# Attention's output projection: upper token tiles finished first, with five weight blocks multiplied ahead

## The chip, the cores and the metric

The kernel runs on one core of one Trainium2 chip. The metric is device time in microseconds (us) for one execution of the whole kernel. Three runs of the kernel before gave 1104.22, 1106.31 and 1106.82 us; their median, 1106.31 us, is the time before.

## What is computed

A trunk of two layers over 512 tokens of width 1024. Each layer is a token mixer and then a SwiGLU feed-forward network (FFN), each between two RMS norms, with a shift, scale and gate that come from a conditioning vector. Layer 0 mixes with a stick-breaking attention, whose output projection `w_o` is the stage of this change:

```python
    for i in range(DEPTH):
        shift, scale, gate = ada_modulation(c, mix_ada_w[i], mix_ada_b[i])
        h = rms_norm(x, mix_pre_g[i]) * (1.0 + scale) + shift
        j = i // N_MIXERS
        if i % N_MIXERS == 0:
            y = stick_breaking_mixer(h, sb_w_qkv[j], sb_w_o[j])
        else:
            y = token_mixing_mixer(h, tm_w_in[j], tm_ln_g[j], tm_w_s[j], tm_b_s[j], tm_w_out[j])
        x = x + gate * rms_norm(y, mix_post_g[i])
        shift, scale, gate = ada_modulation(c, ffn_ada_w[i], ffn_ada_b[i])
        h = rms_norm(x, ffn_pre_g[i]) * (1.0 + scale) + shift
        y = swiglu(h, ffn_w_gate[i], ffn_w_up[i], ffn_w_down[i])
        x = x + gate * rms_norm(y, ffn_post_g[i])
```

## The kernel before

**Numbers.** All is float32. Each operand of a matmul is split into a high part, rounded to the matmul's reduced format, and a low part, the rest. `split` (L128) does this with a copy on ACT (ScalarE) for the high part and a subtraction on DVE (VectorE) for the low one. `mm3` (L120, its matmuls recorded at L109) is the product: high by high, high by low, low by high, three matmuls on PE (TensorE) into one PSUM bank. Weights come by DMA into one of two raw buffers (tile `raw`), and `wemit` splits them into the tiles `wh` and `wl`. A raw buffer is free for the next load once its `wl` is made.

**The ring of weights.** `wget` takes the weights in the fixed order of `stream` and also asks for a few of those behind (its `look`, 3 if nothing else is said). `wtile` gives each a slot in turn: one of five in `wpool`, and, once the attention is over, a sixth in `wpool2`, which is opened only then. Which of the five a tile gets, and when, is for the tile framework's scheduler, which also orders the instructions of each engine where the code doesn't chain them. A slot is written again when the last matmul that reads it is done.

**The projection** (`out_proj`, s=0). The 512 tokens are four tiles of 128, here tile 0 to tile 3; "lower" are tiles 0 and 1, "upper" are 2 and 3. The 1024 rows of `w_o` are eight blocks, here block 0 to block 7. A tile's result needs all eight blocks and lies in two PSUM banks, one for each half of the width (tile `y`). One step is one block, one tile, one half: three matmuls of 512 columns. All eight banks of PSUM hold `y` by the end. As the attention ends with the last of eight head pairs, its generator `filler` puts steps of the projection between its matmuls: `NEARLY` = 4 blocks (0 to 3) for tiles 3 and 2, which are 16 steps, spread by the tables `FILLS` and `LAST`. Then `out_proj` does blocks 0 to 3 for tiles 0 and 1, and then, tile by tile in the order 0, 1, 2, 3, the last four blocks (4 to 7, `J` = 4), and after each tile its boundary.

**The boundary** (`boundary`) of a tile is a chain over three engines: squares of `y` on ACT (`junk`) with their sum, `y` times the gate on DVE (`t<-y,G`), a square root on ACT (`sd`), a reciprocal on DVE, the new `x` on DVE (`x<-t,r,x`), its squares on ACT (`junk<-x`), `x` times the scale on DVE (`t<-x,A`), a second root and reciprocal, the normed row on DVE (`t<-t,r,B`), eight transposes on PE into two banks (`tp`), and for each bank a copy on ACT (`hTh`) and a subtraction on DVE (`hTl`). These two are the FFN's input. For the first two tiles ACT also keeps a plain copy (`c`).

**What follows.** The FFN's first three units (`unit`, f = 0 to 2) are computed for half of the tokens at a time, gate and up, 48 matmuls of 256 columns (tile `gu`). `f0.first()` does the lower half (columns 0 to 255) as soon as tiles 0 and 1 are through; the transposes of the other two tiles stand between these three units. Then come the same three units for the upper half, and then the units f = 3 to 21 as seven products of half size (`seven`; tiles `r1` to `r3`), which read four sums of the input, S1 to S4. `sums` makes all four behind the second pair of tiles, from `c` and from the transposes' banks (`fs` on DVE, `Sh` on ACT, `Sl` on DVE). S1 is the difference of the two halves of the upper tokens' channels; the other three need both halves of the tokens.

Of the kernel before, what the change touches and what calls it, by code (L numbers as in the profile page):

```python
# [13 lines left out]
P = 128  # L14
# [19 lines left out]
def trunk(ctx: ExitStack, tc: tile.TileContext, A: dict, out: bass.AP):  # L34
# [458 lines left out]
    def boundary(s, tt, y, xin, hT, S, tag, mid=None):  # L493
# [26 lines left out]
        for q in range(2):  # L520
# [12 lines left out]
            if S is not None and tt < 2:  # L533
                if tt == 0:
                    S["c", q] = slot(F32, "c", 4, 256)
                act.activation(S["c", q][:, :, tt * P : (tt + 1) * P], a, AF.Copy)
            late.append(a)
        return lambda: sums(S, tt, late)
# [33 lines left out]
    def out_proj(s, nk, get_act, wkey, J, bg, hT, nxt=(), pre=None, S=None, steps=0, bg2=None):  # L572
# [10 lines left out]
        def step(k, tt, a, w, halves=(0, 1)):  # L583
            for hf in halves:
                if k == 0 or k == mid and tt == last:
                    y[tt][hf] = bank("y", "p" if tt == last else "b")
                mm3(
                    y[tt][hf][:],
                    a[0][:, tt * P : (tt + 1) * P], a[1][:, tt * P : (tt + 1) * P],
                    w[0][:, 0, hf * 512 : (hf + 1) * 512],  # L590
                    w[1][:, 0, hf * 512 : (hf + 1) * 512],
                    k == 0 or k == mid and tt == last, k == nk - 1 or k + 1 == mid and tt == last,
                )
# [6 lines left out]
        for k in range(nk - J):  # L600
# [17 lines left out]
        ]  # L618
        sqrt_table()
        xs = {tt: x_load(tt) for tt in range(2)}  # L620
        xin = xs.get
        for tt in range(NT):
            for hf in range(2):
                for k, a, w in tail:
# [5 lines left out]
            if tt < 2:  # L630
                boundary(s, tt, y[tt], xin, hT, S, "p" if last == 0 else "b")
                xs[tt + 2] = x_load(tt + 2)
        evacs, late = [], []
        for n, tt in enumerate((2, 3)):
# [5 lines left out]
            if nxt and tt == 2:  # L640
# [4 lines left out]
                    mid if nxt and tt == 3 else None,  # L645
# [211 lines left out]
    with tc.tile_pool(name="att", bufs=1) as att, tc.tile_pool(name="att2", bufs=2) as att2:  # L857
# [284 lines left out]
    class Ffn:  # L1142
        def __init__(self, s, li, hT, S):
            self.s, self.li, self.hT, self.S = s, li, hT, S
# [29 lines left out]
        def first(self):  # L1174
            return [lambda f=f: self.unit(f, 0, 256, 2) for f in range(NH)]
# [58 lines left out]
        def units(self, bg0):  # L1234
            for f in range(NH):
                self.unit(f, 256, 256)()
# [220 lines left out]
    def gmlp(bg, hT, nhT, nS, nxt):  # L1457
# [219 lines left out]
```

## Time and profile before

| | us |
|---|---|
| runs (median of 3) | 1106.31 (1104.22 to 1106.82) |
| span of the profiled execution, which is its own time here: the profile shows nothing around it | 1104.6 |
| PE busy with matmuls | 1085.9 |
| DVE busy | 945.9 |
| ACT busy | 594.2 |

The last product of the attention ends near 243 us of that span, the projection and its boundaries reach to about 290 us, and the units of seven products begin at 312.4 us. In the lists of instructions the columns are start, duration, engine, line, operation, output and inputs by the program's names, shape, count, and in brackets the idle time just before with what ended it. A duration is longer than the distance to the next instruction of the same engine, since these overlap; where a chain of several is added up, the distance counts.

### The profile page before, as it was taken

To read this page: it belongs to the slowest core of one execution; us is meant where nothing else is said; L and a number is where in the kernel's file an instruction comes from. 1 tells how busy PE (TensorE), PEld (TensorE's weight loads), DVE (VectorE), ACT (ScalarE), POOL (GpSimd) and SP (SyncE) were. 2 spreads that over 40 slices of the span, in tenths; PEclk is the share of its full clock that TensorE was granted. 3 is DMA by queue.
4 is the path that set the end of the run, shared out by engine and by line. 5 is a ranking of instruction groups with operands and counts; after the bars stand their busy time and mean duration, and the time that the engine had idled before them with its cause. 6 is when DMAs were issued, how large, how long until landed. Compare 5 with 4: busy or idle time off the path is not lost.

```text
span 1104.6 us, 18512 instructions
## 1 busy us (share of the span) xinstructions
PE 1085.9 (98%) x7404; PEld 979.0 (89%) x7404; DVE 945.9 (86%) x1248; ACT 594.2 (54%) x982; POOL 29.5 (3%) x53
## 2 busy tenths in 40 slices
PE   6999999999999999999999999999999999999997
PEld 4787788788999999998888889988999999989996
DVE  4988999966989999989866967668979999899997
ACT  6554665665655555554243626426555555565662
POOL 0020100000000000000000000001000000000000
PEclk9999999999999999999999999999999999999999
DMA  8976434304433434359757465334334343333252
GB/s 302 370 226 217 142 116 133 125 11 152 157 112 131 162 119 146 132 197 351 272 191 256 144 205 196 96 116 155 128 117 155 128 159 102 110 115 96 77 187 81
DMA packets 51355, 176.38 MB, mean 160 GB/s; under 512 B 6074, under 2 KB 9146, under 8 KB 51268
## 3 DMA queue, kind: packets, MB, share of 16 engines
q1 hardware_dynamic: 48708, 166.81, 44.6%
q0 software_dynamic: 2560, 8.39, 2.1%
q8 instruction: 58, 0.95, 0.3%
q14 instruction: 29, 0.24, 0.1%
HBM read 164.69 MB, written 8.39 MB: 157 GB/s over the span
## 4 chain that ended last, share of the span: by engine, by line
PE 90%; DVE 4%; DMA 2%; ACT 2%; issue 1%; SPq 0%; DVEq 0%; ACTq 0%
PE r L109 32%; PE y L109 18%; PE pqk L109 7%; PE gu L109 6%; PE v L109 5%; PE X L109 4%; PE u L109 4%; PE Y L109 3%; PE av L109 2%; PE z L109 2%; PE tw L117 1%; PE tp L117 1%; PE Z L109 1%; PE W L109 1%; PE ab L109 1%
## 5 line engine op out<-in xcount | busy, mean ns | idle before, releaser
L87 ACT ACTIVATE wh<-raw 128x1024 fp32r<-128x1024 f32 (+1 forms) x112 | 115.7, 1038 | 130.5 <-PE y L109 39.4
L109 PE MATMUL r<-Sh,wh 128*128 128x256 f32 x608 | 168.1, 276 | 0.5 <-ACT e L87 0.5
L109 PE MATMUL r<-Sh,wl 128*128 128x256 f32 x608 | 167.9, 276 | 0.0
L109 PE MATMUL r<-Sl,wh 128*128 128x256 f32 x608 | 167.9, 276 | 0.0
L109 PE MATMUL y<-wh,as 128*128 128x512 f32 x480 | 149.9, 390 | 0.0
L178 DVE TENSOR_TENSOR wl<-raw,wh 128x1024 fp32r<-128x1024 f32 x87 | 105.8, 1222 | 48.2 <-ACT wh L87 47.6
L109 PEld LDWEIGHTS r<-Sh,wh 128*128 128x128 f32 x608 | 114.1, 188 | 1.0 <-ACT e L87 0.9
L109 PEld LDWEIGHTS r<-Sl,wh 128*128 128x128 f32 x608 | 114.1, 188 | 0.1
L109 PEld LDWEIGHTS r<-Sh,wl 128*128 128x128 f32 x608 | 114.1, 188 | 0.0
L109 PEld LDWEIGHTS y<-wh,as 128*128 128x128 f32 x480 | 90.0, 188 | 18.6
L71 DVE TENSOR_TENSOR wl<-f,wh 128x1024 fp32r<-128x1024 f32 x87 | 103.2, 1220 | 0.0
L87 ACT ACTIVATE wh<-f 128x1024 fp32r<-128x1024 f32 x87 | 91.8, 1055 | 15.3 <-DVE f L71 11.6
L87 ACT ACTIVATE e<-r 128x256 f32<-128x256 f32 x114 | 43.7, 385 | 101.8 <-PE r L109 100.8
L109 PE MATMUL y<-wl,as 128*128 128x512 f32 x240 | 93.7, 391 | 0.0
L109 PE MATMUL r<-hTh,wh 128*128 128x256 f32 x304 | 84.2, 277 | 0.2 <-DVE gu L71 0.2
L109 PE MATMUL r<-hTl,wh 128*128 128x256 f32 x304 | 84.0, 276 | 0.0
L109 PE MATMUL r<-hTh,wl 128*128 128x256 f32 x304 | 84.0, 276 | 0.0
L109 PE MATMUL r<-hTh,b 128*128 128x256 f32 x304 | 57.9, 276 | 0.0
L109 PEld LDWEIGHTS r<-hTh,wh 128*128 128x128 f32 x304 | 57.1, 188 | 0.9 <-DVE gu L71 0.9
L109 PEld LDWEIGHTS r<-hTh,wl 128*128 128x128 f32 x304 | 57.1, 188 | 0.0
L109 PEld LDWEIGHTS r<-hTl,wh 128*128 128x128 f32 x304 | 57.1, 188 | 0.0
L87 ACT ACTIVATE wh<-rawx 128x1024 fp32r<-128x1024 f32 x38 | 40.4, 1063 | 29.8 <-PE r L109 29.0
(262 smaller groups left out, 2937.1 us busy)
## 6 DMA issues: line engine op xcount, KB each, us to landing
rawada<-in_ada SPq DMA_DIRECT2D x80, 512.0 KB, 5.7
rawy<-in_wy SPq DMA_DIRECT2D x38, 512.0 KB, 4.6
rawx<-in_wx SPq DMA_DIRECT2D x38, 512.0 KB, 3.7
raw<-in_wdown SPq DMA_DIRECT2D x22, 512.0 KB, 5.4
raw<-in_wdn SPq DMA_DIRECT2D x22, 512.0 KB, 3.6
raw<-in_wqk SPq DMA_DIRECT2D x16, 512.0 KB, 3.9
ada<-in_ada0p SPq DMA_DIRECT2D x12, 512.0 KB, 6.3
raw<-in_wgu SPq DMA_DIRECT2D x12, 512.0 KB, 3.5
```

What stands on the lines that cost most here:

```text
L71: b = getattr(nc.vector, op)(*args, **kw)
L87: b = nc.scalar.activation(*args, **kw)
L109: b = nc.tensor.matmul(o, l, r, start=start, stop=stop, skip_group_check=True)
L117: last_tp[0] = nc.tensor.transpose(o, i, ident)
L178: last_low[0] = nc.vector.tensor_tensor(l[:], raw[:], h[:].bitcast(F32), ALU.subtract)
```

## The change

The projection of the attention gets a mode `up`.

- `NEARLY` is 5: the attention's last pairs also do block 4 for tiles 3 and 2. That is 20 steps ahead in place of 16, and `LAST` gets four more places.
- `J` is 2, and the order of the tiles is 2, 3, 0, 1. Blocks 4 and 5 are done first (block 4 for tiles 0 and 1 only, where it opens their sums; block 5 for all), then blocks 6 and 7 for tile 2 and for tile 3, and then, for each of tiles 0 and 1, blocks 6 and 7 and behind them blocks 0 to 3 (`early`).
- The FFN's first three units take the upper half of the tokens first (`lo` = 256), the lower half later. The second FFN's stay as they were.
- The plain copies `c` are of the upper tiles. A new `sums_up` makes S1 of a tile right at its upper boundary (one `fs`, one `Sh`, one `Sl`), and S2 to S4 at the lower ones (three of each).

The diff, without its smaller lines:

```diff
+        if lead == (0, 1):
+            return lambda: sums(S, tt, late)
+        return lambda: sums_up(S, tt, late)
+
+    def sums_up(S, tt, a):
+        c = slice(tt % 2 * P, (tt % 2 + 1) * P)
...
+        c0, c1 = [S["c", q][:, :, c] for q in range(2)]
...
+        if tt > 1:
+            dve.tensor_tensor(f[:, 0], c0, c1, ALU.subtract)
+            part("1", f[:, 0])
+            return
...
+        dve.tensor_tensor(f[:, 0], a[0], c0, ALU.subtract)
+        dve.scalar_tensor_tensor(f[:, 1], f[:, 0], -1.0, c1, ALU.mult, ALU.subtract)
+        part("2", f[:, 1])
+        dve.tensor_tensor(g[:, 1], f[:, 1], a[1], ALU.add)
+        part("4", g[:, 1])
+        part("3", f[:, 0])
...
-        for k in range(nk - J):
+        for k in range(npre - 1 if up else 0, nk - J):
...
+        early = [(k, get_act(k), pre["w"][k]) for k in range(npre - 1)] if up else []
         sqrt_table()
-        xs = {tt: x_load(tt) for tt in range(2)}
+        seq = (2, 3, 0, 1) if up else (0, 1, 2, 3)
+        xs = {tt: x_load(tt) for tt in seq[:2]}
         xin = xs.get
-        for tt in range(NT):
+        for n, tt in enumerate(seq):
             for hf in range(2):
-                for k, a, w in tail:
+                for k, a, w in tail + (early if n > 1 else []):
                     step(k, tt, a, w, (hf,))
...
+                if up:
+                    f()
...
-        NEARLY = 4
+        NEARLY = 5
...
-        LAST = (2, 2, 2, 2, 2, 2, 1), (1, 1, 1, 1, 1, 1, 1), (2, 0, 2, 0, 2, 2, 0)
+        LAST = (2, 2, 2, 2, 2, 2, 1), (2, 1, 1, 1, 1, 1, 1), (3, 1, 2, 1, 2, 2, 0)
...
-    f0, f1 = Ffn(1, 0, hT1, S1), Ffn(3, 1, hT3, S3)
+    f0, f1 = Ffn(1, 0, hT1, S1, 256), Ffn(3, 1, hT3, S3, 0)
...
-        4, bg, hT1, f0.first(), early, S1,
+        2, bg, hT1, f0.first(), early, S1, up=True,
```

How this moves instructions is shown at three places. Names carry a number for each tile. Block 4 is `wh_2057` and `wl_2058`, block 5 `wh_2063` and `wl_2064`, block 6 `wh_2069` and `wl_2070` in both kernels; block 7 is `wh_2393` before and `wh_2075` now. The banks of tile 0 are `y_2339` and `y_2343` before, `y_2357` and `y_2361` now; those of tile 1 now `y_2365` and `y_2369`, of tile 2 `y_2255` and `y_2259`, of tile 3 `y_2079` and `y_2111`. `o` is the attention's output, and a bracket names whose counters an instruction waits for.

First place: PE where it goes from block 4 to block 5 behind the attention. Before, block 4 of tile 0 stands behind the 16 steps of blocks 0 to 3 (48 matmuls):

```order
L109 MATMUL y_2339<-wl_2058,o_1905 128x512
L109 MATMUL y_2339<-wh_2057,o_1905 128x512
L109 MATMUL y_2339<-wh_2063,o_2102 128x512 [waits Activation_49]
L109 MATMUL y_2339<-wl_2064,o_2102 128x512 [waits DVE_49]
L109 MATMUL y_2339<-wh_2063,o_2102 128x512
L109 MATMUL y_2339<-wh_2069,o_2240 128x512 [waits Activation_49]
L109 MATMUL y_2339<-wl_2070,o_2240 128x512 [waits DVE_49]
L109 MATMUL y_2339<-wh_2069,o_2240 128x512
L109 MATMUL y_2339<-wh_2393,o_2324 128x512 [waits Activation_49]
L109 MATMUL y_2339<-wl_2394,o_2324 128x512 [waits DVE_49]
```

Now the four steps of block 4 (12 matmuls) stand alone between the attention and block 5; this is their end and the start of block 5:

```order
L109 MATMUL y_2369<-wl_2058,o_1905 128x512
L109 MATMUL y_2369<-wh_2057,o_1905 128x512
L109 MATMUL y_2357<-wh_2063,o_2108 128x512 [waits Activation_49]
L109 MATMUL y_2361<-wh_2063,o_2108 128x512
L109 MATMUL y_2365<-wh_2063,o_2108 128x512
L109 MATMUL y_2369<-wh_2063,o_2108 128x512
L109 MATMUL y_2255<-wh_2063,o_2108 128x512
L109 MATMUL y_2259<-wh_2063,o_2108 128x512
L109 MATMUL y_2357<-wl_2064,o_2108 128x512 [waits DVE_49]
```

Blocks 5, 6 and 7 are now each done for all four tiles one after the other (24 matmuls of block 5, 24 of block 6), with six matmuls by `wh` ahead of the first one by `wl`, where before one tile went through blocks 4 to 7 at a time; blocks 0 to 3 of tiles 0 and 1 come last.

Second place: ACT, which makes these blocks' `wh`, behind the attention's last output `o`. Before (`wh_2399` is the FFN's first weight):

```order
L87 ACTIVATE o_2324<-of_2319 128x512 [waits DVE_49]
L87 ACTIVATE wh_2063<-raw_2061 128x1024 [waits DMAHW2_49,PE_49]
L87 ACTIVATE wh_2069<-raw_2067 128x1024 [waits DMAHW3_49,PE_49]
L87 ACTIVATE wh_2393<-raw_2391 128x1024 [waits DMAHW6_49,PE_49]
L87 ACTIVATE wh_2399<-raw_2397 128x1024 [waits DMAHW7_49,PE_49]
L87 ACTIVATE junk,sq_2438<-y_2339 128x512 [waits PE_49]
```

Now:

```order
L87 ACTIVATE o_2342<-of_2337 128x512 [waits DVE_49]
L87 ACTIVATE wh_2063<-raw_2061 128x1024 [waits DMAHW2_49,PE_49]
L87 ACTIVATE wh_2069<-raw_2067 128x1024 [waits DMAHW3_49,DVE_49,PE_49]
L87 ACTIVATE wh_2075<-raw_2073 128x1024 [waits DMAHW6_49,DVE_49,PE_49]
L87 ACTIVATE junk,sq_2426<-y_2255 128x512 [waits PE_49]
```

The counter of PE that the copy of block 5 waits for stood for the last matmul of block 0 before and stands for the last matmul of block 4 now. The copy of block 6 waited for block 1's last and waits for block 5's last; that of block 7 waited for block 2's and waits for block 6's.

Third place: DVE between the normed row of the first finished tile and that of the second. Before (tile 0, then tile 1):

```order
L71 SCALAR_TENSOR_TENSOR t_2440<-t_2440,r_2458,B_1198 128x1024 [waits DVE_49]
L71 TENSOR_TENSOR t_2512<-y_2347,G_458 128x512 [waits Activation_49]
L71 TENSOR_SCALAR ss_2516<-sq_2510 128x1
L71 TENSOR_TENSOR t_2512<-y_2351,G_458 128x512 [waits Activation_49]
L71 TENSOR_TENSOR hTl_2468<-tp_2462,hTh_2467 128x4x128 [waits Activation_49]
L71 RECIPROCAL r_2520<-sd_2518 128x1 [waits Activation_49]
L71 SCALAR_TENSOR_TENSOR x_2412<-t_2512,r_2520,x_2412 128x1024 [waits DMAHW5_49,DVE_49]
L71 TENSOR_TENSOR hTl_2479<-tp_2473,hTh_2478 128x4x128 [waits Activation_49]
L71 TENSOR_TENSOR t_2512<-x_2412,A_676 128x1024 [waits DVE_49]
L71 RECIPROCAL r_2530<-sd_2528 128x1 [waits Activation_49]
L71 SCALAR_TENSOR_TENSOR t_2512<-t_2512,r_2530,B_1198 128x1024 [waits DVE_49]
```

Now (tile 2, then tile 3; the rows from the second `hTl` of tile 2 on; `wl_2376` and `wl_2406` are the FFN's first two weights):

```order
L71 TENSOR_TENSOR hTl_2467<-tp_2461,hTh_2466 128x4x128 [waits Activation_49]
L71 TENSOR_TENSOR fs_2476<-c_2459,c_2470 128x512 [waits Activation_49]
L71 TENSOR_TENSOR t_2494<-y_2079,G_458 128x512 [waits DVE_49]
L71 TENSOR_TENSOR t_2494<-y_2111,G_458 128x512
L71 TENSOR_TENSOR Sl_2475<-fs_2476,Sh_2474 128x4x128 [waits Activation_49]
L71 SCALAR_TENSOR_TENSOR x_2412<-t_2494,r_2502,x_2412 128x1024 [waits DMAHW5_49,DVE_49]
L178 TENSOR_TENSOR wl_2376<-raw_2373,wh_2375 128x1024 [waits DMAHW7_49,Activation_49]
L178 TENSOR_TENSOR wl_2406<-raw_2403,wh_2405 128x1024 [waits DMAHW0_49,Activation_49]
L71 TENSOR_TENSOR t_2494<-x_2412,A_676 128x1024 [waits DVE_49]
L71 RECIPROCAL r_2512<-sd_2510 128x1 [waits Activation_49]
L71 TENSOR_SCALAR ss_2677<-sq_2671 128x1 [waits Activation_49]
L71 SCALAR_TENSOR_TENSOR t_2494<-t_2494,r_2512,B_1198 128x1024 [waits DVE_49]
```

The second tile's `t<-y,G` stood ahead of the first tile's `hTl` and stands behind both of them and behind the new `fs` of S1; `Sl` of S1 and two weights' `wl` have come between. On PE, the transposes of the second tile had 17 matmuls of `y` between them and the first of the FFN, and now have none; 35 matmuls of `y` stand between the first tile's transposes and the second's, where 25 stood.

More of the change, by code (lines that the diff above doesn't have):

```diff
@@ L584, in step @@
             for hf in halves:
-                if k == 0 or k == mid and tt == last:
+                if k == (npre - 1 if up else 0) or k == mid and tt == last:
                     y[tt][hf] = bank("y", "p" if tt == last else "b")
@@ L591, in step @@
                     w[1][:, 0, hf * 512 : (hf + 1) * 512],
-                    k == 0 or k == mid and tt == last, k == nk - 1 or k + 1 == mid and tt == last,
+                    k == (npre - 1 if up and tt < 2 else 0) or k == mid and tt == last,
+                    k == (npre - 2 if up and tt < 2 else nk - 1) or k + 1 == mid and tt == last,
                 )
@@ L1174, in first @@
         def first(self):
-            return [lambda f=f: self.unit(f, 0, 256, 2) for f in range(NH)]
+            return [lambda f=f: self.unit(f, self.lo, 256, 2) for f in range(NH)]
         def seven(self, f, pending, bg0):
```

39 lines of the change are left out of this document (24 added, 15 removed).

## The prediction

> **What bounds the kernel now.** I read the page's busy shares first, then what PE waited for over the whole span, then two stretches by engine, then the chain of work that ended last around the projection.
>
> ```profile
> PE 1085.9 (98%) x7404; PEld 979.0 (89%) x7404; DVE 945.9 (86%) x1248; ACT 594.2 (54%) x982; POOL 29.5 (3%) x53
> ```
>
> ```profile
> PE tp L117 <- DVE x L71: 8.7, 2, 7.8
> ...
> PE av L109 <- DVE ar L71: 0.8, 1, 0.8
> PE r L109 <- ACT e L87: 0.5, 1, 0.5
> PE av L109 <- ACT ar L87: 0.4, 1, 0.4
> ```
>
> PE is busy for 98% of the span, and the list of its waits (us in total, times, longest) says that the rest is its start (8.7) and little else. Three waits lie near this change: 0.8 and 0.4 in the attention's last pairs, 0.5 in the first unit of seven products. They are all that a better order can win here. Everything else that moves time must be a new wait.
>
> The stretches show who is close behind (us, then busy us of PE, its loads, DVE, ACT):
>
> ```profile
> 257.00:290.00 33.00, 32.95 (x205) 28.90 (x204) 29.25 (x44) 23.21 (x49) 3.12 (x5) 1.00 0.48 165
> ...
> 312.40:500.00 187.60, 187.11 (x1621) 185.68 (x1621) 169.65 (x224) 105.32 (x178) 1.92 (x2) 1.00 0.42 147
> ```
>
> In the boundaries DVE is busy 29.25 of 33 us: PE's matmuls cover its chains, with little to spare. In the units PE idles 0.49 us in 187.6, so time that PE loses earlier isn't given back there.
>
> ```profile
> 243.42 22.23 PE y L109 x98
> 265.68 1.09 PE tp L117 x8
> ...
> 277.46 5.71 PE gu L109 x48
> 283.18 0.87 PE tp L117 x8
> ...
> 290.63 21.88 PE gu L109 x192
> ```
>
> The chain through the projection is PE alone. It gives PE's rates: 22.23/98 = 0.227 us for a matmul of y, 0.87 for the eight transposes of a tile, 5.71 for one of the FFN's first units.
>
> **The change: matmuls ahead.** No matmul is added. Four steps (12 matmuls) go into the attention's last pairs. The step behind the wait of 0.8 gets 0.68 us of new cover (3 x 0.227), that behind the wait of 0.4 gets two steps: of 1.2 us 1.1 are gone. **-1.1.**
>
> **The change: four blocks in one slot.** Blocks 0 to 3 are kept to the end, so four of the five slots are taken while the attention lasts, and blocks 4 to 7, all asked for by then (the last look is 3 beyond block 4), follow one another in the fifth. The order says so too: each copy waits for the last matmul of the block before it, and behind that matmul PE has nothing but this block. Before, the slots came from blocks 0 to 3, with other steps to do. Rows of PE, ACT and DVE of before for one such turn:
>
> ```profile
> 233.73 0.33 PE L109 MATMUL av<-ar,U 128*128 128x128 f32 x1 [0.42 <-ACT ar L87]
> ...
> 245.76 0.62 PE L109 MATMUL y<-wh,o 128*128 128x512 f32 x2
> ```
>
> ```profile
> 233.09 1.05 ACT L87 ACTIVATE ar<-tw,oneb 128x384 fp32r<-128x384 f32 x2
> ...
> 246.19 1.07 ACT L87 ACTIVATE wh<-raw 128x1024 fp32r<-128x1024 f32 x1 [0.28 <-PE y L109]
> ...
> 254.77 1.06 ACT L87 ACTIVATE wh<-raw 128x1024 fp32r<-128x1024 f32 x1 [1.44 <-DMA raw<-in_wgu]
> ```
>
> ```profile
> 247.29 1.23 DVE L178 TENSOR_TENSOR wl<-raw,wh 128x1024 fp32r<-128x1024 f32 x1 [0.33 <-ACT wh L87]
> 250.00 1.23 DVE L178 TENSOR_TENSOR wl<-raw,wh 128x1024 fp32r<-128x1024 f32 x1 [1.49 <-ACT wh L87]
> ```
>
> Block 0's last matmul started at 245.76 and the copy into its slot at 246.19, 0.43 later. PE could start another matmul 0.23 after it, so 0.2 is lost before the copy. The copy takes 1.07. PE follows about 0.1 behind (the first of two `ar`, half of 1.05, ends near 233.63; `av` starts at 233.73). That is 1.37 us for each of blocks 5, 6, 7. The `wl` (ready 0.03 + 1.23 + 0.1 after the copy) is covered by six matmuls by `wh` (1.36). Raw data are no limit: block 7's load starts when block 5's `wl` is made, and one load takes 3.5 us (250.00 + 1.23 to 254.77), against two blocks' 10.9 us of matmuls. **3 x 1.37 = +4.1.**
>
> **The change: boundaries with less cover.** DVE and ACT are idle through those waits, and the first boundary starts late. I follow the chain with time 0 at block 7's first matmul, by distances between starts in before's first boundary:
>
> ```profile
> 259.79 0.60 ACT L87 ACTIVATE junk<-y 128x512 bf16<-128x512 f32 x1 [2.03 <-PE y L109]
> ...
> 262.62 1.06 ACT L87 ACTIVATE junk<-x 128x1024 bf16<-128x1024 f32 x1 [1.82 <-DVE x L71]
> ...
> 263.81 0.29 ACT L87 ACTIVATE sd<-sx,epsb 128x1 f32<-128x1 f32 x1
> ...
> 266.37 0.60 ACT L87 ACTIVATE hTh<-tp 128x512 fp32r<-128x512 f32 x1 [0.45 <-PE tp L117]
> ...
> 267.72 0.60 ACT L87 ACTIVATE c<-tp 128x512 f32<-128x512 f32 x1 [0.57 <-DVE hTl L71]
> ```
>
> ```profile
> 261.30 1.28 DVE L71 SCALAR_TENSOR_TENSOR x<-t,r,x 128x1024 f32<-128x1024 f32 x1
> 262.62 1.23 DVE L71 TENSOR_TENSOR t<-x,A 128x1024 f32<-128x1024 f32 x1
> ...
> 264.33 1.28 DVE L71 SCALAR_TENSOR_TENSOR t<-t,r,B 128x1024 f32<-128x1024 f32 x1
> 265.53 0.68 DVE L71 TENSOR_TENSOR t<-y,G 128x512 f32<-128x512 f32 x1
> ...
> 267.00 0.69 DVE L71 TENSOR_TENSOR hTl<-tp,hTh 128x512 fp32r<-128x512 f32 x1
> ...
> 277.68 2.35 DVE L178 TENSOR_TENSOR wl<-raw,wh 128x1024 fp32r<-128x1024 f32 x2
> ...
> 298.69 1.29 DVE L71 TENSOR_TENSOR fs<-fs,c 128x512 f32<-128x512 f32 x2
> ```
>
> Each further instruction in a queue on DVE costs 0.6 (512 wide: 1.29 less 0.69), 1.12 (1024 wide: 2.35 less 1.23) or 1.2 (the kind with a column: 264.33 to 265.53). From the second `junk<-y` to the transposes it is 5.89 (259.79 to 265.68), from `x` 4.38 (261.30 to 265.68), from the transposes to `hTh` 0.69, from there to `hTl` 0.63, from `hTl` to `c` 0.72.
>
> Tile 2: its banks are complete with the 8th and 10th matmul; the second `junk` starts at 2.6, a little behind the first, and the transposes at 8.6. PE has 37 matmuls for that time (8.4). **+0.2.**
>
> Tile 3: tile 2's transposes run to 9.45, then 35 matmuls to 17.4. DVE: `hTl` 9.9; the second `hTl` waits for `c` and `hTh` (about 0.6 each on ACT), 11.8; `fs` waits for the second `c`, 13.1; two `t<-y,G`, `Sl`: `x` at 15.5; two `wl`, 16.7 and 17.8; `t<-x,A` 18.95; the reciprocal and `ss`; the normed row 20.3; transposes 21.65. **+4.3.** Before, this tile's `t<-y,G` ran while ACT copied, and no `wl` and no `fs` lay between.
>
> First unit of the FFN: transposes to 22.5. The third `wh` waits for its raw buffer (`wl` at 16.7 + 1.2, load 3.5: 21.5) and holds up `hTh` on ACT until 22.5; its `wl` holds up `hTl` on DVE until 23.8; PE's second matmul starts at 24.55. The same again for the second half costs 0.3. Before, 17 matmuls of y covered this. **+2.2.**
>
> Tile 0: that unit ends at 30.4. DVE: second `hTl` 25.5, `c` 26.2, `fs` 26.85, two `t<-y,G`, `Sl`, `x` 29.25, transposes 4.38 later, 33.6. **+3.2.** Tile 1: second unit to 40.2; DVE is free of tile 0's row at 33.5, then `ss` and two `t<-y,G`, two `hTl`, reciprocal, `fs`, `x` at 36.95; 4.38, and 0.95 for a weight's copy that ACT does ahead of the root: 42.3. **+2.1.** The third unit's `wl` is 0.1 late. **+0.1.** After that 21.9 us of units (the last chain row) lie ahead of the products, and the S1 work already done (four instructions of 0.6 on DVE) no longer lies there: the wait of 0.5 goes. **-0.5.** The moved S1, the swapped halves and the loads of `x` (landed long before) have no other price.
>
> Sum: -1.1 + 4.1 + 0.2 + 4.3 + 2.2 + 3.2 + 2.1 + 0.1 - 0.5 = +14.6. The profiled execution has 1104.6, so 1119.2 by its clock; the median of the runs lies 1.7 above it: **1121 us** (+1.3%). A measurement of this kernel can tell about 0.3% (3.3 us) from no change.
>
> The unknown is how much of the boundaries' 12.1 (+0.2 to +0.1 above) appears. Nothing of it can fall below the turn from transposes to the first unit (0.69 + 0.63 + 0.69 + 0.1, less 0.87 of the transposes and 0.12 for one matmul of the unit: 1.1), since no other matmul stands there. Upwards, each hand-over between engines could be 0.2 longer; the chain has some 25, so +5. I take the chain as added up, since DVE's queue alone, without any hand-over, makes two thirds of it (tile 3: 8.9 of the 13.1 us from tile 2's row to its own).
>
> **Rivals.** *The boundaries stay covered*: what I let wait for `c`, for the copies or for loads is early, and of 12.1 only 0.2 and 1.1 remain: 1106.3 - 1.1 + 4.1 + 1.3 - 0.5 = 1110. For it: before shows no wait there at all. Against: the four extra instructions in DVE's queue ahead of tile 3's row (`fs`, `Sl`, two `wl`) are 3.4 us. It holds if tile 3's row is ready 17 us behind block 7's first matmul. Chance 0.12.
>
> *PE's clock falls in the long wait.* At the end of the kernel the granted clock (the column before the DMA share) stays at 1.00 for 3.5 us behind the end of the last matmul and then falls to half:
>
> ```profile
> 1097.14 0.39 PE L109 MATMUL Y<-wh,al 128*128 128x512 f32 x1
> ```
>
> ```profile
> 1100.00:1101.00 1.00, 0.00 (x0) 0.00 (x0) 0.99 (x2) 0.00 (x0) 0.00 (x0) 1.00 0.00 0
> 1101.00:1102.00 1.00, 0.00 (x0) 0.00 (x0) 0.00 (x0) 0.00 (x0) 0.00 (x0) 0.53 0.43 146
> ```
>
> ```profile
> 7.84 1.97 PE L117 MATMUL tp<-identt,x 128*128 128x128 f32 x8 [7.84 <-DVE x L71]
> ```
>
> The wait of 4.3 us is longer than 3.5. Behind it, the transposes would take 1.97 (as at the start, behind 7.84 us of idling) in place of 0.87, half of it on the path to `hTh`, and a part of the first unit's 5.71 would double; 3.2 of that is hidden, since tile 0's row is late anyway. That leaves 0.5 to 2.5: about 1122.5. Chance 0.10. [...]
>
> *DVE, not PE, sets the end*, and PE's lost time comes back in the units: then only DVE's work counts, which is the same in number and has 2.4 us done earlier; 1105, not slower. It decides if PE waits 14 us or more in the units of before; it waits 0.5. Chance 0.04.
>
> **How the numbers follow.** My forecast has 0.74, with 1115 to 1126 of its own (half of the 12.1 less, or the +5). The clock's case lies inside; of the covered case the range takes in the upper part: 1111 to 1126. Faster only by the last rival's edge: 0.02. Within 0.3%: 0.04, which holds the rest of it and part of the covered case near 1109. Slower: 0.94.
>
> **What would show it.** Right: three waits of PE's y for ACT's `wh` of 1.2 to 1.5 us; waits of `tp` for DVE's `t` of 4.3, 3.2, 2.1 and of `gu` for `hTl` near 2; no waits of 0.8 and 0.4 in `av`; the units of seven products starting some 15 us later. Wrong: y running through blocks 4 to 7 without idling; `tp` without waits; or the products starting late but the end not moving.

## The result, and the profile after

| | before | after |
|---|---|---|
| median of the runs, us | 1105.26 (4 runs) | 1121.19 (4 runs) |
| range, us | 1104.01 to 1106.82 | 1119.54 to 1122.22 |
| span of the profiled execution, us | 1104.6 | 1120.5 |
| granted clock, mean | 0.998 | 0.993 |

The changed kernel takes 1.0136 times as long, with a 95% interval of 1.0123 to 1.0149. Between the medians, and between the two spans, lie 15.9 us, where the prediction's sum had 14.6. Every run lasts some 1.7 us longer than its span (1122.22 and 1120.5 for the profiled one), so the span is not the whole time of a run. The engines' work is as before, but for 5 us on PE:

```profile
PE 1091.1 (97%) x7404; PEld 982.5 (88%) x7404; DVE 946.3 (84%) x1248; ACT 594.3 (53%) x982; POOL 29.5 (3%) x53
```

What PE waited for (us in total, times, longest):

```profile
PE tp L117 <- DVE x L71: 8.2, 2, 7.5
PE tp L117 <- DVE t L71: 7.4, 3, 4.0
PE y L109 <- ACT wh L87: 3.4, 3, 1.1
PE gu L109 <- DVE hTl L71: 0.8, 1, 0.8
PE av L109 <- DVE accl L71: 0.7, 1, 0.7
PE gu L109 <- ACT hTh L87: 0.5, 1, 0.5
```

The waits of 0.8 and 0.4 for `ar` and that of 0.5 for `e` have gone. Three waits of `y` for `wh`, three of `tp` for `t` and two of `gu` have come, of the kinds foretold; their sizes are compared further down. The wait for `accl` has nothing to do with the change: it lies 95 us into the span, and comes back below.

The stretches (us, busy us of PE, its loads, DVE, ACT, POOL, then granted clock, DMA share, GB/s):

```profile
257.00:290.00 33.00, 26.53 (x118) 21.28 (x117) 20.36 (x30) 17.36 (x35) 1.09 (x2) 0.88 0.42 144
```

```profile
281.00:282.00 1.00, 0.00 (x0) 0.00 (x0) 1.00 (x2) 0.61 (x3) 0.00 (x0) 0.88 0.98 283
...
284.00:292.00 8.00, 6.71 (x29) 6.01 (x29) 5.59 (x8) 4.77 (x7) 0.00 (x0) 0.50 0.53 171
292.00:293.00 1.00, 1.00 (x11) 1.00 (x10) 1.00 (x2) 0.00 (x0) 0.00 (x0) 1.00 0.19 78
...
302.24:305.65 3.41, 1.54 (x14) 1.35 (x14) 2.76 (x4) 3.39 (x6) 1.01 (x2) 1.00 0.37 154
305.65:309.06 3.41, 3.41 (x19) 3.41 (x17) 3.41 (x6) 2.00 (x5) 0.00 (x0) 0.50 0.49 153
```

```profile
329.60:517.20 187.60, 187.60 (x1627) 186.22 (x1626) 167.66 (x220) 105.55 (x178) 1.92 (x2) 1.00 0.42 146
329.60:1120.50 790.90, 783.27 (x5660) 732.74 (x5658) 681.81 (x906) 412.14 (x657) 10.55 (x15) 1.00 0.44 153
```

In the boundaries PE is busy for 26.53 of 33 us where it was 32.95, and DVE for 20.36 where it was 29.25: both wait, in turn. The clock is at half from about 281.8 (0.88 is 0.76 us at full speed and 0.24 at half) to 292.0, and again from 305.7 to 309.1. The units of seven products begin at 329.6 and not at 312.4, 17.2 us later. In their first 187.6 us PE no longer idles at all, and from their start to the end it takes 790.9 us where it took 792.3 (312.35 to 1104.62): of what was lost, 1.4 us come back there.

The chain of work that ended last, behind the attention, shows the shared slot: block, copy, block, copy.

```profile
244.34 2.78 PE y L109 x12
...
247.15 1.07 ACT wh L87
...
248.25 5.75 PE y L109 x24
...
254.03 1.06 ACT wh L87
```

PE behind the last `y` (start, us, then in brackets the idle time ahead of it and what ended it), and DVE from tile 2's second `hTl` to tile 3's normed row:

```profile
279.37 0.39 PE L109 MATMUL y<-wh,o 128*128 128x512 f32 x1
283.78 1.97 PE L117 MATMUL tp<-identt,t 128*128 128x128 f32 x8 [4.02 <-DVE t L71]
286.25 0.58 PE L109 MATMUL gu<-hTh,wh 128*128 128x256 f32 x1 [0.50 <-ACT hTh L87]
287.63 0.58 PE L109 MATMUL gu<-hTl,wh 128*128 128x256 f32 x1 [0.80 <-DVE hTl L71]
...
295.05 0.28 PE L109 MATMUL gu<-hTh,wl 128*128 128x256 f32 x1
296.83 1.07 PE L117 MATMUL tp<-identt,t 128*128 128x128 f32 x8 [1.51 <-DVE t L71]
```

```profile
273.89 0.69 DVE L71 TENSOR_TENSOR hTl<-tp,hTh 128x512 fp32r<-128x512 f32 x1 [1.15 <-ACT hTh L87]
275.24 0.69 DVE L71 TENSOR_TENSOR fs<-c,c 128x512 f32<-128x512 f32 x1 [0.66 <-ACT c L87]
275.85 1.28 DVE L71 TENSOR_TENSOR t<-y,G 128x512 f32<-128x512 f32 x2
...
277.65 1.28 DVE L71 SCALAR_TENSOR_TENSOR x<-t,r,x 128x1024 f32<-128x1024 f32 x1
278.85 2.36 DVE L178 TENSOR_TENSOR wl<-raw,wh 128x1024 fp32r<-128x1024 f32 x2
281.12 1.22 DVE L71 TENSOR_TENSOR t<-x,A 128x1024 f32<-128x1024 f32 x1
...
282.44 1.28 DVE L71 SCALAR_TENSOR_TENSOR t<-t,r,B 128x1024 f32<-128x1024 f32 x1
```

The reader should see two things in the last view. `fs` waits 0.66 for `c`, and tile 3's `t<-y,G` (275.85) begins only when `fs` is done and behind both of tile 2's `hTl`. Further on, two `wl` stand between `x` and `t<-x,A` of tile 3's row. Which of these is the cause can't be read here; the experiments tell.

### The profile page after: what moved, and what is told of

The parts are those of the page before. It is cut to its first block, busy times and chain, and to the rows that moved or that the text cites. A ratio compares the mean times of both kernels' runs of the same rounds, so it can differ in the third digit from the quotient of the medians.

```text
span 1120.5 us, 18515 instructions
## 1 busy us (share of the span) xinstructions
PE 1091.1 (97%) x7404; PEld 982.5 (88%) x7404; DVE 946.3 (84%) x1248; ACT 594.3 (53%) x982; POOL 29.5 (3%) x53
## 4 chain that ended last, share of the span: by engine, by line
PE 85%; DVE 6%; DMA 4%; ACT 2%; issue 2%; SPq 0%; DVEq 0%; ACTq 0%
PE r L109 31%; PE y L109 16%; PE pqk L109 7%; PE gu L109 5%; PE v L109 4%; PE X L109 4%; PE u L109 4%; PE Y L109 3%; PE av L109 2%; PE z L109 2%; PE tw L117 1%; DMA rawada<-in_ada 1%; PE Z L109 1%; PE W L109 1%; PE tp L117 1%
```

## The experiments

All ratios are to before, run on the same chip. The theory at the start was the prediction's: the slot costs about 4 us, the late start and DVE's longer queue in the boundaries about 12, the attention's part gains 1 to 2. The rivals were single causes (the slot alone, S1 alone, the weights alone, the clock) and a loss in the attention's part itself.

**The attention's part alone.**

```diff
-    f0, f1 = Ffn(1, 0, hT1, S1, 256), Ffn(3, 1, hT3, S3, 0)
+    f0, f1 = Ffn(1, 0, hT1, S1, 0), Ffn(3, 1, hT3, S3, 0)
...
-        2, bg, hT1, f0.first(), early, S1, up=True,
+        3, bg, hT1, f0.first(), early, S1,
```

> Only the attention's part of the change: five blocks ahead for the upper token tiles and the new numbers in the attention's last pairs. Behind it the blocks run in their own order, tiles 0 and 1 first, three blocks in the tail, S1 where it was before. Theory (the attention's part is a gain; all of the loss is made behind it, by the slot and by the boundaries): the two waits of 0.8 and 0.4 us in av are gone, nothing new comes in the boundaries, and the end is about 1.8 us earlier than before: ratio 0.998, about 1103.5. Rival (the twelve matmuls moved forward were the cover of the boundaries, so that moving them costs there what it gains): ratio 1.000 or above, with a new wait of tp or gu of 1 us or more. Rival (the new attention itself costs, since a fifth weight copy lies among its work): ratio above 1.001.

Measured: 1106.99 us, 1.0013 (1.0005 to 1.0022). Not the theory. The waits for `ar` are gone, but the boundaries have new ones:

```profile
PE tp L117 <- DVE t L71: 0.8, 1, 0.8
PE tp L117 <- DVE ss L71: 0.8, 1, 0.8
PE gu L109 <- DVE hTl L71: 0.7, 1, 0.7
```

But the edit had a second part: with five blocks ahead of it, the tail is three blocks and not four. So:

**The shorter tail alone**, in the kernel before.

```diff
-        4, bg, hT1, f0.first(), early, S1,
+        3, bg, hT1, f0.first(), early, S1,
```

> The kernel before, with one number changed: a tail of three blocks and not of four, so that 18 matmuls and not 24 lie between the ends of two tiles. The run with the attention's part alone needed that too (its fifth block lies ahead of the tail), and was 1.1 us slower than before, with waits of 0.8, 0.8, 0.7 and 0.3 in the boundaries. Theory (the twelve matmuls moved into the attention were the boundaries' cover): the shorter tail alone costs nothing, ratio 0.999 to 1.001, no waits of tp or gu. Rival (the tail is what costs, and the attention's 1.8 us are a gain): waits of 2 us or more in the boundaries, ratio 1.002 to 1.004.

Measured: 1108.09 us, 1.0012 (1.0003 to 1.0021). Two of the three waits are there without any matmul moved:

```profile
PE tp L117 <- DVE t L71: 0.8, 1, 0.8
...
PE gu L109 <- DVE hTl L71: 0.7, 1, 0.7
```

So the tail costs, as the rival said, if less than its bounds (1.5 us of waits, 1.0012), and by this comparison only the wait of 0.8 for `ss`, of the three, is the price of the moved matmuls. The two kernels end level within their intervals: with this tail the attention's part brings nothing that can be measured, and a version with it alone is no gain over before.

**A sixth slot** in the changed kernel: blocks 5, 6 and 7 are asked for only when the second pool of weights is open.

```diff
-            w = pre["w"][k] if k < npre else wget(wkey(k))
+            w = pre["w"][k] if k < npre else wget(wkey(k), 1 if up else 3)
...
+        if up:
+            turn[0] = 4
...
-            early["w"].extend(wget(("wo", k)) for k in range(NEARLY))
+            early["w"].extend(wget(("wo", k), min(3, NEARLY - 1 - k)) for k in range(NEARLY))
...
+    turn[0] = 4
```

> The changed kernel, but blocks 5, 6 and 7 are asked for only when the weights' second pool is open, so that block 5 goes into a slot of its own, 6 into that of block 4 and 7 into that of block 5. The boundaries' order is untouched. Theory (two separate causes, the slot for 4 us, the boundaries' chain for about 11): the three waits of y for wh (3.4 us in all) go to about 1 or less, and the end is 3 to 4 us earlier than the changed kernel: ratio to before 1.010 to 1.011, about 1117; the waits of tp for t stay at 4.0, 1.5, 1.9 within 0.7. Rival (the slot is the root of all: DVE and ACT stand still through those waits and the first boundary starts late): the waits of tp shrink too, and 8 us or more of the 15 come back: ratio 1.006 or less. Rival (the slot costs nothing on its own, since what is won in it is lost in the boundaries, which DVE's row sets): ratio 1.013 to 1.014 as the changed kernel.

Measured: 1112.68 us, 1.0063 (1.0049 to 1.0077): 8.5 us less than the changed kernel by the medians, more than double the 3.4 us of the three waits. The waits of `y` are gone, and so are two of the three of `tp`; the third, tile 0's, is longer:

```profile
PE tp L117 <- DVE t L71: 5.6, 1, 5.6
```

The rival that makes the slot the root named 8 us or more and a ratio of 1.006 or less: the 8 us are there, and the ratio lies at its edge. The slots' waits push the first boundary back (tile 2's transposes start at 263.5 here, at 270.7 in the changed kernel), so they cost more than themselves. They are not all: 7 us remain.

**S1 of the upper tiles late.**

```diff
+        ups = []
...
-                if up:
-                    f()
+                ups.append(f)
...
-            for f in late:
+            for f in (ups if up else []) + late:
                 f()
```

> The changed kernel, but the S1 work of the upper tiles (a subtraction and a split: fs and Sl on DVE, Sh on ACT, for tiles 2 and 3) is issued behind the last boundary, as the other S1 work is, and not behind each upper boundary. Theory (tile 3's row is late by DVE's queue, in which fs and Sl are two of four extra instructions of 0.6 to 0.7 us each): tile 3's wait falls by about 1.3, from 4.0 to 2.7; tile 1's falls by 0 to 1.3 for its own fs; the wait of 0.5 in the first unit of seven products comes back: the end is 1 to 2 us earlier: ratio 1.012, about 1119.5. Rival (S1 at the upper boundaries is the cause of the boundaries' loss): 5 us or more come back, ratio 1.009 or less. Rival (PE's clock: the wait behind tile 3 is what makes it fall): with 2.7 us the clock doesn't fall at 282 us, and the clock of the whole run is 0.996 or more.

Measured: 1114.24 us, 1.0088 (1.0071 to 1.0106): 7 us back, not 1 to 2. The rival holds. Tile 3's wait is not 1.3 us shorter, it is gone. In DVE's queue `t<-y,G` of tile 3 stands ahead of tile 2's `hTl` again, as in the kernel before. Two instructions of 0.7 us don't explain that; the order does. What had turned it? `t` and `fs` are both tiles of one pool with two buffers (tag `n`). Tile 2's `t` has one, `fs` takes the other, and so tile 3's `t` can only be written when tile 2's transposes have read its own `t`. The expectation also had the wait of 0.5 in the first unit of seven products come back; it didn't.

**The weights late.**

```diff
-            (k, get_act(k), wget(wkey(k), J + 1 if k == nk - J else 0))
+            (k, get_act(k), wget(wkey(k), (J - 1 if up else J + 1) if k == nk - J else 0))
```

> The changed kernel, but the FFN's first weights are asked for block by block and not ahead of the tail of two blocks, so that their wh and wl stand behind tile 3's row in the queues of ACT and DVE and not ahead of it. Theory (two wl of 1.2 us stand ahead of tile 3's row on DVE): tile 3's wait falls from 4.0 to about 1.7, but the weights then come later for the FFN's first unit (copies 2.4 us later, the load of the third that waits for the first's wl too): its wait rises by 1 to 2.5, so that the end moves by -1.5 to +1: ratio 1.012 to 1.015. Rival (the loss in the boundaries is all from weights ahead of rows): 4 us or more come back: ratio 1.010 or less. Rival (the clock): no fall of the clock at 282 us, as the wait is shorter than 3.5 us, and the first unit's matmuls take 0.12 us and not 0.21.

Measured: 1119.70 us, 1.0131 (1.0114 to 1.0148): the total as the theory had it, but not for its reason. Only one of the two `wl` has left its place ahead of `t<-x,A`, the other stands ahead of the row's last instruction, and tile 3's wait is 3.9 us as before. The clock falls all the same: the first unit's matmuls start 0.21 us apart, and 0.12 from 292.0 on. The run doesn't tell what the two `wl` are worth, only that asking later doesn't help.

**`fs` in another buffer.** All S1 work stays where the change put it.

```diff
         if tt > 1:
-            dve.tensor_tensor(f[:, 0], c0, c1, ALU.subtract)
-            part("1", f[:, 0])
+            f = slot(F32, "fs", 4, 256)[:, :, :P]
+            dve.tensor_tensor(f, c0, c1, ALU.subtract)
+            part("1", f)
             return
+        f = npool.tile([P, 2, 4, P], F32, tag="n", name=nm("fs"))
```

> The changed kernel, but the difference fs of the upper tiles is written to a buffer of the 28 common ones and not to one of the two that the normed rows t use. All S1 instructions stay at the upper boundaries. Theory (buffers: fs takes the second of two buffers, so that tile 3's row can begin only when tile 2's transposes have read its own, and stands in DVE's queue behind them): tile 3's row begins near 270 us and not at 275.85, its wait of 4.0 goes to below 1, the clock doesn't fall at 282, and the end is 5 to 8 us earlier, like the run with S1 late: ratio to before 1.006 to 1.009. Rival (queue, as the prediction put it: fs, Sl and the weights' wl are four more instructions ahead of the row): the wait stays at 2.7 or more, ratio 1.012 to 1.014.

Measured: 1114.50 us, 1.0078 (1.0065 to 1.0091): 6.7 us back, as with S1 late. DVE between the two rows:

```profile
268.24 1.28 DVE L71 SCALAR_TENSOR_TENSOR t<-t,r,B 128x1024 f32<-128x1024 f32 x1
269.44 0.68 DVE L71 TENSOR_TENSOR t<-y,G 128x512 f32<-128x512 f32 x1
...
270.90 0.69 DVE L71 TENSOR_TENSOR hTl<-tp,hTh 128x512 fp32r<-128x512 f32 x1
...
274.68 0.69 DVE L71 TENSOR_TENSOR fs<-c,c 128x512 f32<-128x512 f32 x1
...
276.05 1.27 DVE L71 SCALAR_TENSOR_TENSOR t<-t,r,B 128x1024 f32<-128x1024 f32 x1
```

Tile 3's `t<-y,G` follows tile 2's row at once, at 269.44 and not at 275.85, and `fs` stands behind it. Its normed row starts at 276.05 and not at 282.44, and tile 3's wait is gone. The buffer alone is thus enough to make tile 3 late. The run doesn't part it from the queue, since the order followed it: `Sl` and the two `wl`, which stood ahead of this row in the changed kernel, stand behind it here (from 277.24 on). Between the two rows lie 7.8 us in place of 13.1; of the 5.3, those three instructions are some 2.9 (0.6 and 2.27 by the distances in the changed kernel), the rest is mostly DVE standing idle before tile 2's `hTl` and `fs`. What is left is a wait ahead of tile 0's transposes, and the clock falls behind it (0.50 from 291 to 294 us):

```profile
PE tp L117 <- DVE ss L71: 3.8, 1, 3.8
```

**Sixth slot and S1 late.** The edits of the two runs together.

```diff
+            w = pre["w"][k] if k < npre else wget(wkey(k), 1 if up else 3)
...
+                ups.append(f)
```

> The sixth slot and the late S1 of the upper tiles together. Theory (two causes with one part in common: the slots cost 3.4 us on their own, and either edit makes tile 3's wait of 4.0 and the fall of the clock go): the end is 3 to 6 us earlier than with S1 late alone: ratio 1.004 to 1.006, about 1111. Rival (two separate causes): both gains add up, ratio 1.001 to 1.003. Rival (DVE's row now sets the boundaries, and nothing in the slots matters any more): ratio 1.006 to 1.009.

Measured: 1108.77 us, 1.0020 (1.0008 to 1.0031). The ratio lies in the range of the two separate causes. By the ratios, each to before on its own chip, the two edits gain 0.0073 and 0.0048, and together 0.0116, which is 0.6 us short of their sum and well inside the intervals. By the medians, which come from runs on different chips, they gain 8.5 and 7.0 and together 12.4, 3.0 us less than their sum. So the causes are mostly separate; a common part, of which tile 3's wait would be the likely one since either edit takes it away, isn't shown.

**The long wait filled** in the changed kernel, to keep the clock up.

```diff
+            if up and n == 3:
+                k, a, w = early[-1]
+                for _ in range(18):
+                    mm(y[tt][1][:], a[0][:, tt * P : (tt + 1) * P], w[1][:, 0, 512:1024], False, True)
```

> The changed kernel with 18 more matmuls of 0.227 us on PE between the last matmul of y and tile 3's transposes, where PE waited 4.0 us. They add block 3's product of wl and o 18 more times to tile 1's second half, whose output so differs. Theory (the clock's fall costs little, since tile 0's row is late anyway): the clock stays at 1.00 from 282 to 292 us, the first unit takes about 5.7 us and not 8.8, the wait for tile 0 grows from 1.5 to 3.5 or more, no second fall follows at 305 us or one that costs as much as before; the end moves by 0 to -2 us: ratio 1.012 to 1.014. Rival (the clock is the size of the whole loss behind tile 3): 4 us or more come back, ratio 1.010 or less. Rival (the matmuls delay what DVE and ACT do for tiles 0 and 1): the end is later, ratio 1.015 or more.

Measured: 1120.28 us, 1.0128 (1.0113 to 1.0142). As the theory had it, the first unit runs at full clock and PE waits longer for tile 0 (2.8, not quite the 3.5 expected); the clock falls behind that wait instead.

```profile
PE tp L117 <- DVE t L71: 3.7, 2, 2.8
```

```profile
284.00:292.00 8.00, 5.58 (x47) 5.15 (x46) 6.23 (x9) 4.78 (x7) 0.00 (x0) 1.00 0.49 167
...
296.00:299.00 3.00, 2.91 (x14) 2.94 (x15) 2.23 (x5) 1.38 (x3) 0.00 (x0) 0.52 0.00 0
```

PE does 47 matmuls where it did 29 in the same 8 us, and the end hardly moves: DVE's row for tile 0 sets it. The fill doesn't free the kernel of falls, it leaves one of 3.4 us (from 296.2); but a first unit at full clock moves the end by only 0.9 us, within the intervals.

**Slot and buffer**, both causes taken away: the sixth slot, and `fs` in another buffer.

```diff
+            w = pre["w"][k] if k < npre else wget(wkey(k), 1 if up else 3)
...
+            f = slot(F32, "fs", 4, 256)[:, :, :P]
```

> The sixth slot, and the difference fs of the upper tiles in another buffer; S1 stays at the upper boundaries. Theory (slots and buffers are all that the change costs; what is left of it is the attention's 1.8 us and 0.5 us in the first unit of seven products): the waits of tp for tiles 3, 0 and 1 add up to 2 us or less, ratio 0.998 to 1.002. Rival (the order itself, the upper tiles first with four blocks behind them, leaves the boundaries uncovered): waits of 4 us or more remain, ratio 1.004 or more.

Measured: 1107.74 us, 1.0015 (1.0006 to 1.0023). The ratio is inside the theory's bounds: by the medians 13.5 us are back, and 1.6 stay against before on the same chip. One wait is left, ahead of tile 1's transposes; with 2.4 us it is a little over the 2 that the theory allowed. These are the first profile's rows:

```profile
PE tp L117 <- DVE x L71: 7.5, 2, 7.3
PE tp L117 <- DVE t L71: 2.4, 1, 2.4
```

The twelve runs go from 1104.2 (the profiled one) to 1109.9, wider than before's.

**S1 of the lower tiles behind the last row**, an attempt to shorten that wait.

```diff
-            for f in late:
-                f()
+            with tc.issue_after(feature[0].ins):
+                for f in late:
+                    f()
```

> The kernel with the sixth slot and the other buffer, and the S1 work of the lower tiles (fs and what follows) issued only behind tile 1's normed row. In the run before this one PE waited 2.4 us for that row, with two fs of 0.6 us in DVE's queue ahead of it; and eleven of its twelve runs took 1106.3 to 1109.9 us, most at a clock of 0.997, while the profiled one took 1104.2 at 0.999. Theory (the two fs are on the path, and the wait of 2.4 us is what lets the clock fall in most runs): the wait falls to about 1.2, the clock is 0.998 or 0.999 in most runs, and the median is 1102.5 to 1105: ratio to before 0.996 to 0.999, the first version at or ahead of before. Rival (the sd that tile 1's row waits for on ACT sets it, not DVE's queue): the wait stays at 2 us or more, ratio 1.000 to 1.002. Rival (the spread has nothing to do with the wait): wait shorter, but times up to 1110 and clocks of 0.997 as before, ratio 1.000 to 1.002.

Measured: 1111.58 us, 1.0052 (1.0039 to 1.0065). My theory fell: the wait is still 2.0, and a new one has come behind it:

```profile
289.27 1.09 PE L117 MATMUL tp<-identt,t 128*128 128x128 f32 x8 [2.00 <-DVE t L71]
293.15 0.55 PE L109 MATMUL gu<-hTh,wh 128*128 128x256 f32 x1 [2.79 <-DVE act L71]
```

Without the two `fs`, DVE idles 1.09 us for ACT's `sd` in that row, so ACT's queue holds it, as the first rival said of the wait, though not of the time (1.000 to 1.002). Why the third unit now waits for `act` is not shown. Two other runs in which sums were made late have that wait too (2.77 with S1 late, 2.91 with the sixth slot and S1 late); that `fs` reads the transposes' banks later, and so keeps them, is likely but only argued.

**Slot and buffer, the wait filled**, to see whether the spread is the clock.

```diff
+                if up:
+                    k, a, w = early[-1]
+                    for _ in range(9):
+                        mm(y[tt][1][:], a[0][:, tt * P : (tt + 1) * P], w[1][:, 0, 512:1024], False, True)
```

> The kernel with the sixth slot and the other buffer, and nine more matmuls of 0.227 us (2.04 us) in PE's wait of 2.4 us ahead of tile 1's transposes; they write to a bank whose content has been used, so that nothing of the output changes. With them two wl on DVE change places, which may cost up to 1.1 us at the third unit. Theory (the wait lets the clock fall, and that makes the spread of the runs): no run at 0.997 or below, all within 1104 to 1107, median 1105 to 1106: ratio 0.999 to 1.000. Rival (the spread is not the clock at this wait): some runs at 1108 or more, median 1107.5 to 1109: ratio 1.0015 to 1.003.

Measured: 1108.17 us, 1.0021 (1.0012 to 1.0031). All twelve runs have a clock of 0.998 or 0.999 (most had 0.997 without the fill), so the wait does let it fall. But they go from 1105.1 to 1109.6 all the same: the spread is not only the clock, and the rival's times hold. The swapped `wl` cost 0.9 in this profile, which hides part of what the clock gave.

**Slot and buffer once more**, unchanged, for a second profile.

> The kernel with the sixth slot and the other buffer once more, unchanged, for a second profile: its first profile has 1104.2 us with one wait of 2.4, the median of its runs is 1107.7. Theory (what the typical run has more are further waits in the same boundaries, since a load there lands later in some runs): 1106 to 1109 us, and a wait in the boundaries that the first profile doesn't have. Rival (what differs lies elsewhere in the kernel): the same one wait of 2.4 us, and the boundary ends at the same time.

Measured: 1107.27 us. The rival holds: the boundaries have the same one wait.

```profile
PE tp L117 <- DVE x L71: 8.7, 2, 7.7
PE tp L117 <- DVE t L71: 2.4, 1, 2.4
```

The 3.1 us between the two profiles (spans 1102.4 and 1105.5) lie in two places: tile 1's transposes start 1.6 us later (288.36 and 289.94), most of it from the wait at the very start (7.5 and 8.7), and the clock is at half for 3.4 us (290.39 to 293.80) behind a wait of the same 2.4 us, which costs the other half. Why it fell here and not in the first profile, the last section shows. A third source showed in other profiles, again far from the change:

```profile
97.07 0.67 PE L109 MATMUL av<-accl,ones 128*128 128x512 f32 x1 [1.97 <-DVE accl L71]
```

That wait was 1.97 in the profile with the shorter tail, where the clock went to half behind it (97.25 to 100.66), 0.7 in the changed kernel and absent before. It is why single profiles of this kernel are not compared to better than about 2 us here.

No version beat the kernel before.

## Why the prediction was right, and where it wasn't

The time (1121.0 against 1121.2) is right, and the mechanisms were there in kind: new waits, and little time given back. Some of the agreement is luck. The sum had 14.6 us and 15.9 were measured; but before's median, to which the sum was added, fell from 1106.31 to 1105.26 with a fourth run, which makes up for most of it. In the profiles, the way from the attention's `v` to the first of the seven products grew by 16.8 us beside the wait for `accl`, where the terms had 15.1, and 1.4 us came back behind it, where they had 0.5.

- **Matmuls ahead, -1.1.** Right. From the last matmul ahead of `v` (43.76 before, 43.43 now) to the last stretch of `y` (243.42, 244.34) the trace has 199.7 us before and 200.9 now. Behind that point before has 140 matmuls of `y` (98, 25 and 17 between the transposes) and the changed kernel 132, so eight more stand ahead of it and not twelve: four of blocks 0 to 3 for tiles 0 and 1 already stood there. These eight are 1.8 us and the wait for `accl` is 0.7, which leaves a gain of 1.3, and the waits for `ar` are 1.2 of it. That the gain is worth nothing by itself, with a tail of three blocks, was not foreseen.
- **Four blocks in one slot, +4.1.** The waits themselves are right: 1.53 from one matmul to the next, three times, less 0.23 each: 3.9. What the slot is worth is more, 6.8 to 8.5 us by the runs, since the waits also start the boundaries late. The prediction had the second part, among the boundaries' terms.
- **Tile 2's transposes, +0.2.** Right (270.72, 0.2 behind the last matmul).
- **Tile 3's transposes, +4.3.** The size is right: 4.41 us between two starts, less the 0.23 of a matmul, 4.2. The reason given is only the near one. I put it down to a longer queue: "no `wl` and no `fs` lay between", and in the rivals "the four extra instructions in DVE's queue", 3.4 us. That queue is what the changed kernel has; but with `fs` and `Sl` both kept and only the buffer changed, the order turns back and the wait is gone. I had followed the new order, which has `t<-y,G` behind the transposes, to the right time, but never asked why the order was so. It was the second buffer of the pool.
- **First unit, +2.2.** It was 2.9, since the third weight's load took 4.48 us where I had 3.5 from before's rows, at a DMA share of 0.98 in the microsecond from 281. That weight's copy on ACT starts at 284.66 and `hTh` follows it at once, at 285.62; the transposes took 1.97 and not 0.87 at half clock, but mostly beside this copy:

```profile
280.10 4.48 DMA raw<-in_wgu
```

- **Tile 0, +3.2.** Its wait is 1.51, but the unit ahead of it ran at half clock and took 1.9 more; together 3.4 to 3.6.
- **Tile 1, +2.1.** Right: 1.87, and 0.15 of hand-over.
- **Third unit, +0.1.** Here the second fall of the clock lies, 3.4 us at half: from tile 1's transposes to the products it is 24.3 us where it was 22.8, 1.5 us that the sum doesn't have.
- **The wait of 0.5 for `e`.** It is gone, but the reason (S1 done earlier) is not borne out: it is absent too where S1 is made late, and in the run with the shorter tail, where S1 wasn't moved at all. The way from the products to the end is 0.8 to 1.4 us shorter than before's in every other profile, that one's (791.3) included, so nothing shows this part to be the change's.

As to the rivals: the fall of the clock, which I had as a rival, is no rival but a part of what happened, beside the forecast's waits. Its first fall was hidden, as that rival's working said of 3.2 us; its second was not in it. The covered boundaries (1110) didn't come about in the changed kernel, but nearly so in the run with slot and buffer, which has one wait of 2.4 left and no longer pays for the slot (1107.7): it is those two, and not the upper tiles going first, that lay the boundaries bare. DVE as the bound (1105) found no support: PE idles nowhere in the units.

So the shared slot and the shared buffer make 13.5 us, and 1.6 stay: one wait of 2.4 and, in most runs, some 1.5 for the clock behind it, less the attention's 1.3 and the 1 us behind the products' start. That last balance is worked out from profiles and isn't shown by a run of its own.

## What to carry to other kernels

When work is moved earlier, look up which pool each of its scratch tiles comes from: a tile that takes the second of two buffers can turn the order of a whole queue, and moving it to another pool can be worth as much as moving the work back (6.7 and 7.0 us here). A queue's order names the place but not the reason, so ask of each instruction that changed its place what it had to wait for. And blocks that are kept for later keep their slots: count the slots that are left for those between.

## What was unexpected of the hardware

The clock fell behind shorter waits than the 3.5 us that the prediction had read from the end of before's trace. It went to half behind 4.02 us of waiting, but also behind 2.4 (the second profile of slot and buffer), 2.8 (the filled wait, ahead of tile 0), 1.97 (the wait for `accl` with the shorter tail) and, in the changed kernel, 1.87. In the first profile of slot and buffer the same 2.4 us passed without it.

In the changed kernel's trace the clock falls at 281.76, is back at 292.00, falls again at 305.65 and is back at 309.06. The distances are 10.24, 13.65 and 3.41 us, which is three, four and one times 3.413 us (27.30 us from the first point to the last, divided by eight). The two profiles of slot and buffer, cut into stretches of this length from the points where their clock changes (second profile, then first; us, then busy us of PE, with the clock ahead of the DMA share):

```profile
286.98:290.39 3.41, 0.96 (x9) 0.77 (x8) 2.76 (x4) 3.39 (x6) 0.97 (x2) 1.00 0.37 154
290.39:293.80 3.41, 3.41 (x18) 3.41 (x17) 3.41 (x6) 1.97 (x5) 0.00 (x0) 0.50 0.51 144
```

```profile
284.17:287.58 3.41, 1.82 (x17) 1.62 (x15) 2.76 (x5) 3.07 (x5) 1.50 (x2) 1.00 0.42 174
287.58:290.99 3.41, 2.63 (x22) 2.62 (x23) 3.41 (x4) 3.08 (x6) 0.00 (x0) 1.00 0.20 29
```

In the second profile the whole wait lies in one stretch, PE idles 2.45 of 3.41 us there, and the next stretch runs at half. In the first, the wait is cut in two (1.59 and 0.78 us of idling), and the clock stays. In all fourteen profiles, cut in the same way up to the end of PE's work, each of the nine stretches at full clock with 1.87 us of idling or more was followed by half clock (1.87 is the changed kernel's second fall), and none with 1.84 or less was (1.84 came in the run with the weights late). Once down, it stayed at half behind every stretch with 1.0 us of idling or more (2.03 and 1.30 in the changed kernel), and came back behind those with none. So in these profiles it was not the length of a wait alone that went with a fall, but how much of it lay in one such stretch. That is read from profiles of nearly one kernel; no run was made to test it.

What a fall cost differed with the place. In the second profile of slot and buffer, where PE was the chain, the 3.4 us at half cost 1.5 us. The first and longer fall in the changed kernel (10.2 us) cost almost nothing, since the row that PE would have waited for was late anyway: filling the wait ahead of it moved the end by 0.9 us, within the intervals.
